# Convolution sums and gates of the odd layer kept in SBUF instead of DRAM, and the order of two key buffers swapped

## The chip, the cores and the metric

The kernel runs on one core of one Trainium2 chip. The metric is the device time of one execution in microseconds (us), the median of several runs. The profile beside it is of one execution of its own. Its engines are PE (TensorE, matmul), DVE (VectorE), ACT (ScalarE), POOL (GpSimd) and SP (SyncE, which here issues most DMA transfers, in the order of its own queue). Every engine runs its instructions in the order in which the program has them for that engine.

## What is computed

The reference is a backbone of two layers over 1024 latent tokens and 256 context tokens of width 1024. Layer 0 is attention. Layer 1, which the change touches, has two parallel branches: a convolution module and a neighbourhood attention. Cut to the convolution branch:

```
cv, cgl, cg, dq, dk, dv, dg = split_cols(h_lat @ w_in, ODD_WIDTHS)     # 7 x 512 columns
u = val * sigmoid(glu_gate)                                            # cv, cgl
u = conv(u, dw_w, 31 taps, depthwise, padding 15) + dw_b
u = silu(layer_norm(u, ln_g, ln_b))                                    # over the 512 channels
oc = u * silu(silu_gate)                                               # cg
...
od = neighbourhood attention of dq, dk, dv over a 16 x 64 grid, 8 heads, with context keys
y_lat = concatenate([oc, od * silu(dg)]) @ w_out
```

The result is x + gate * y_lat, normalised once more.

## The kernel before

Matrix products in 32-bit precision are made of three passes each: every operand is split into a high part (a cast on ACT) and a low part (a subtraction on POOL or DVE), and `mm3` (L327 to L329) multiplies high by high, low by high and high by low. A weight block is loaded raw by SP (L346, `wr`), cast on ACT (`wh`, L307) and split on POOL (`wl`, L310). Two raw slots serve a block of four pieces, so that pieces three and four can be loaded only when POOL has split pieces one and two.

Channels lie on the 128 partitions, tokens along the free axis. The 512 channels of the convolution are four tiles i = 0 to 3; the latent tokens are two chunks of 512.

Layer 1 runs in these stages.

- **Convolution stage** (pool `cv`). For each i, `conv_proj` multiplies for value, GLU gate and SiLU gate of both chunks. The gated value goes to `U` (1024 tokens and 15 zeros on each side); the SiLU gate goes through `silu2` (Tanh on ACT, one product on DVE) into `sgc`, and from there to the DRAM tensor `Gc` (L1050). `conv_steps` runs beside the matmuls (`pump`): 23 taps as multiply-adds on DVE in PSUM (`cps`), 8 taps on ACT and POOL (`cacc2`, `ptmp`), then a sum into `cacc`, the bias on ACT (L1073) and a store to the DRAM tensor `Uc` (L1074). After the four `conv_proj` comes `d_proj(0)`, the queries, keys, values and gate of the first two attention heads, whose results are stored to DRAM (`QD`, `KD`, `VD`, `GD`).
- **Normalisation stage** (pool `ln`). `ln_steps` normalises one chunk of 512 tokens over the 512 channels: it loads `uc` (4 tiles, 1 MB) from `Uc` (L1081), adds the four tiles on POOL (L1084 to L1086), gets the mean by a matmul with a constant (`mu`, L1091), subtracts it (L1095), squares and adds, gets the reciprocal root by two small groups of matmuls (`trs` and `bc`, L254 and L264), scales, applies SiLU (L1110 to L1114), loads the gate `gc` from `Gc` (L1109), multiplies (L1115) and stores to the DRAM tensor `Oc` (L1116). It runs beside the matmuls of `d_proj(1)`.
- **Attention stage** (pools `d0` and `d1`), woven with `d_proj(2)`, `d_proj(3)` and the output projection. `k_tiles` makes two pairs of key buffers: `KA`, loaded by DMA from `KD` (L384, L385), and `KB`, of which POOL sets four rows to 1.0 (L379) and ACT fills 64 rows by a copy out of `KA` (L390). Scores are a product with `KA` (L491) and one with `KB` (L495).

**What sets the order.** The program text gives each instruction a priority, by its place; the order on each engine is then made when the program is built, by a model of the time at which each instruction is ready. An instruction that is ready may go ahead of one with a higher priority that isn't. On the chip the order is fixed.

**Places in SBUF.** Pools are laid out as a stack, and inside a pool the tiles lie in the order of their first use. `cv` and `ln` begin at the same place, one after the other, and `d0` and `d1` follow at the same place again. A tile that takes the place of older ones waits for the last use of each of these. Bytes of one partition: `cv` 44,032 (taps 512, four U of 4,224, od_cs weights 14,336, cacc2, ptmp and cacc 4,096 each); `ln` with two uc of 8,192 and two gc of 2,048 within it; `d0` 34,880; each `KA` and `KB` 6,144. In layer 0 that part of the memory holds, among others, the residual stream `x1` of the output projection, in three chunks.

Of the kernel before, what the change touches and what calls it, by code (L numbers as in the profile page):

```python
# [10 lines left out]
F32 = mybir.dt.float32  # L11
F32R = mybir.dt.float32r
ALU = mybir.AluOpType
# [5 lines left out]
P = 128  # L19
DK = 8  # L20
NCTX = 256
NLAT = 1024
# [65 lines left out]
def tile_kernel(ctx: ExitStack, tc: tile.TileContext, a, out):  # L88
# [22 lines left out]
    def nm(s):  # L111
        uid[0] += 1
        return f"{s}_{uid[0]}"

    def dram(name, shape, dt=F32):
        return dp.tile(shape, dt, tag=name, name=name)
# [245 lines left out]
    def silu2(psrc, dst):  # L362

        SC.activation(dst, psrc, AF.Tanh, scale=0.5)
        VE.scalar_tensor_tensor(dst, dst, 1.0, psrc, op0=ALU.add, op1=ALU.mult)
# [8 lines left out]
            GP.memset(V[:, :, 128:192].bitcast(F32), 1.0)  # L374

    def k_tiles(pool, n, bufs=1):
        KA = pool.tile([P, n * P], F32R, tag="KA", name=nm("KAt"), bufs=bufs)
        KB = pool.tile([P, n * P], F32R, tag="KB", name=nm("KBt"), bufs=bufs)
        GP.memset(KB[64:68, :].bitcast(F32), 1.0)  # L379
        Ks.append((KA, KB))  # L380

# [608 lines left out]
    lng = const("lng", [P, 4])  # L990
    lnb = const("lnb", [P, 4])
    fg = const("fg", [P, DK])
    Gc = dram("Gc", [P, 4, NLAT])
    Oc = dram("Oc", [P, 4, NLAT])
    Uc = dram("Uc", [P, 4, NLAT])
    QD = [dram(f"QD{i}", [P, 2, 2, 512]) for i in range(4)]
    KD = [dram(f"KD{i}", [P, 2, 12 * P]) for i in range(4)]
    VD = [dram(f"VD{i}", [P, 12, 2, P]) for i in range(4)]
# [2 lines left out]
    with ExitStack() as l1x:  # L1001
# [11 lines left out]
        def half(name, tag="half"):  # L1013
            return lp.tile([P, 512], F32, tag=tag, name=nm(name), bufs=HALF[tag])
# [20 lines left out]
        def conv_proj(vp, i, U):  # L1035
            GP.memset(U[:, 0:15], 0.0)
            GP.memset(U[:, NLAT + 15 : NLAT + 30], 0.0)
            w = [load_w(wp, a["od_cv"], i, 256, WB), load_w(vp, a["od_cs"], i, 128, CWB // 2)]
            for c in (1, 2):
                t0, n = CHUNKS[c]  # L1040
                o = t0 - 256
                pv_ = yield from proj1(*w[0], 0, c)
                pg = yield from proj1(*w[0], 1, c)
                th = half("thc")
                SC.activation(th, pg, AF.Tanh, scale=0.5)
                VE.scalar_tensor_tensor(U[:, 15 + o : 15 + o + n], th, 1.0, pv_, op0=ALU.add, op1=ALU.mult)
                sg = half("sgc", "hf")
                pp = yield from proj1(*w[1], 0, c)
                silu2(pp, sg)
                SY.dma_start(Gc[:, i, o : o + n], sg)  # L1050

        def conv_steps(vp, i, U):
            ps2 = [bank("st", nm("cps")) for _ in range(2)]
            acc2 = vp.tile([P, NLAT], F32, tag="cacc2", name=nm("cacc2"), bufs=1)
            for k in range(31):
                u, w = U[:, k : k + NLAT], taps[:, i, k : k + 1]
                if k % 4 == 3:
                    t = acc2 if k == 3 else vp.tile([P, NLAT], F32, tag="ptmp", name=nm("ptmp"), bufs=1)
                    SC.activation(t, u, AF.Identity, scale=w)
                    if k > 3:  # L1060
                        GP.tensor_tensor(acc2, acc2, t, op=ALU.add)
                    continue
                for c, pc in enumerate(ps2):
                    uc = u[:, c * 512 : (c + 1) * 512]
                    if k == 0:
                        VE.tensor_scalar(pc, uc, w, None, op0=ALU.mult)
                    else:
                        VE.scalar_tensor_tensor(pc, uc, w, pc, op0=ALU.mult, op1=ALU.add)  # L1068
                yield
            acc = vp.tile([P, NLAT], F32, tag="cacc", name=nm("cacc"), bufs=1)  # L1070
            for c, pc in enumerate(ps2):
                VE.tensor_tensor(acc[:, c * 512 : (c + 1) * 512], pc, acc2[:, c * 512 : (c + 1) * 512], op=ALU.add)
            SC.activation(acc, acc, AF.Identity, bias=dwb[:, i : i + 1], scale=0.5)  # L1073
            SY.dma_start(Uc[:, i, :], acc)  # L1074
            yield

        def ln_steps(vp, c):

            cs = slice(c * 512, (c + 1) * 512)
            uc = vp.tile([P, 4, 512], F32, tag="uc", name=nm("uc"), bufs=2)  # L1080
            SY.dma_start(uc, Uc[:, :, cs])  # L1081
            s1 = vp.tile([P, 512], F32, tag="s1", name=nm("s1"), bufs=2)
            s2 = vp.tile([P, 512], F32, tag="s2", name=nm("s2"), bufs=1)
            GP.tensor_tensor(s1, uc[:, 0], uc[:, 1], op=ALU.add)  # L1084
            GP.tensor_tensor(s2, uc[:, 2], uc[:, 3], op=ALU.add)
            GP.tensor_tensor(s1, s1, s2, op=ALU.add)  # L1086
            yield
            for _ in range(2):
                yield
            mu = bank("st", nm("mu"))  # L1090
            PE.matmul(mu, ones5, s1, start=True, stop=True)  # L1091
            SC.copy(s2, mu)
            yield
            for i in range(4):
                VE.tensor_tensor(uc[:, i], uc[:, i], s2, op=ALU.subtract)  # L1095
                if i == 0:
                    SC.activation(s1, uc[:, i], AF.Square)
                else:
                    sq = vp.tile([P, 512], F32, tag="sql", name=nm("sql"), bufs=2)
                    SC.activation(sq, uc[:, i], AF.Square)  # L1100
                    VE.tensor_tensor(s1, s1, sq, op=ALU.add)
                yield
            yield
            bc = yield from rstd_steps(vp, [s1], 512, "st", 2.0)
            SC.copy(s2, bc)
            yield
            for i in range(4):
                gc = vp.tile([P, 512], F32, tag="gc", name=nm("gc"), bufs=2)
                SY.dma_start(gc, Gc[:, i, cs])  # L1109
                VE.scalar_tensor_tensor(uc[:, i], uc[:, i], lng[:, i : i + 1], s2, op0=ALU.mult, op1=ALU.mult)  # L1110
                th = vp.tile([P, 512], F32, tag="sql", name=nm("thl"), bufs=2)
                SC.activation(th, uc[:, i], AF.Tanh, scale=0.5, bias=lnbh[:, i : i + 1])
                VE.tensor_scalar(uc[:, i], uc[:, i], lnb[:, i : i + 1], None, op0=ALU.add)
                VE.scalar_tensor_tensor(uc[:, i], th, 1.0, uc[:, i], op0=ALU.add, op1=ALU.mult)  # L1114
                VE.scalar_tensor_tensor(uc[:, i], uc[:, i], 0.25, gc, op0=ALU.mult, op1=ALU.mult)  # L1115
                SY.dma_start(Oc[:, i, cs], uc[:, i])  # L1116
                yield

        def d_proj(i):
# [33 lines left out]
            for c in VORD:  # L1153
# [20 lines left out]
                for k0 in range(0, len(blocks), 4):  # L1174
# [11 lines left out]
                    while k < len(bl):  # L1186
# [3 lines left out]
                        SY.dma_start(VD[i][:, bl[k][0] : bl[k][0] + e - k], sv[:, k:e].bitcast(F32))  # L1190
                        k = e

        with tc.tile_pool(name="cv", bufs=1, reuse_waits="tile") as vp:
            stg[0] = vp
            taps = const("taps", [P, 4, 31], SY, vp)
# [17 lines left out]
        with tc.tile_pool(name="ln", bufs=1, reuse_waits="tile") as vp:  # L1213
# [12 lines left out]
            for _ in bg:  # L1226
                pass

        dlow = l1x.enter_context(tc.tile_pool(name="d0", bufs=1, reuse_waits="tile"))
        yo = dlow.tile([P, 3, 2, 512], F32, tag="yo", name="yo")  # L1230
        dpool = l1x.enter_context(tc.tile_pool(name="d1", bufs=1, reuse_waits="tile"))
# [362 lines left out]
```

## Time and profile before

| | |
|---|---|
| median of 3 runs | 1579.01 us (1578.08 to 1581.34) |
| the profiled execution | 1581.59 us |
| its span, first to last instruction | 1579.8 us |
| mean granted TensorE clock | 0.962 |
| DMA traffic | 208.23 MB, 132 GB/s on average |
| convolution stage | about 973 to 1137 us |
| normalisation stage | about 1137 to 1226 us |

The profile's page gives each engine's busy time; views of the trace group instructions by line, tile or stretch of time. In a waits view a line reads "engine, what it ran, <- what it waited for: us in total, times, longest". A granted clock of 1.00 is TensorE's full speed. A timeline's line is: start, us, engine, line, operation, what it writes and reads, count, and in brackets the idle time before it with what ended it. Names lose their digits there: the trace calls the tiles `s1` and `s2` both `s`, `p1` is `p`, `cacc2` is `cacc`.

### The profile page before, as it was taken

Reading aid. Unit: us, or ns where it says so; the run is one execution under the profiler, and the core shown is the slowest. Engines: PE = TensorE matmul, PEld = TensorE weight load, DVE = VectorE, ACT = ScalarE, POOL = GpSimd, SP = SyncE. Lnnn points to the kernel's source line nnn. Section 1 sums busy time; section 2 is a strip of 40 time slices with the busy share of each in tenths; the row PEclk is TensorE's granted clock in tenths of the full one; section 3 lists DMA queues with packets and bytes.
Section 4 is the critical chain, followed back from the end, with each engine's and each line's share of the span. In section 5 each row is a group of like instructions: output and inputs, shape, how many; then the busy total and the mean of one; then the engine's idle time right before and its main releaser. Section 6 shows DMA issues by size and latency. Waiting matters only on the chain.

```text
span 1579.8 us, 21684 instructions
## 1 busy us (share of the span) xinstructions
PE 1469.3 (93%) x7084; PEld 1172.7 (74%) x7084; DVE 1086.9 (69%) x2279; ACT 748.8 (47%) x1418; POOL 794.1 (50%) x637
## 2 busy tenths in 40 slices
PE   6899999998998999999999879999989999989995
PEld 2785987886886767876766657888877878768874
DVE  2833576588589865566677856999738466787866
ACT  3722333443435555447556654433334355554563
POOL 3531352553445666557556754664532244364665
PEclk8899999998999999999999989999999999979997
DMA  9473324422312253222112022222595577967632
GB/s 367 151 238 127 114 84 153 137 76 90 110 44 82 87 195 129 64 57 62 41 30 88 7 66 77 86 68 72 175 271 194 186 215 218 284 191 231 187 110 107
DMA packets 158105, 208.23 MB, mean 132 GB/s; under 512 B 15068, under 2 KB 96168, under 8 KB 157992
## 3 DMA queue, kind: packets, MB, share of 16 engines
q1 hardware_dynamic: 151328, 195.27, 39.1%
q10 hardware_dynamic: 6664, 11.57, 2.2%
q8 instruction: 56, 0.92, 0.3%
q14 instruction: 57, 0.47, 0.1%
HBM read 152.27 MB, written 53.22 MB: 130 GB/s over the span
## 4 chain that ended last, share of the span: by engine, by line
PE 73%; DVE 15%; DMA 6%; ACT 2%; issue 2%; POOL 1%; SPq 0%; ACTq 0%; DVEq 0%; POOLq 0%
PE p L327 6%; PE p L328 6%; PE p L329 6%; PE ov L447 4%; PE ov L449 4%; PE po L327 4%; PE po L329 4%; PE po L328 4%; PE ov L448 4%; PE st L491 4%; PE st L495 4%; PE pq L327 3%; PE pq L328 3%; PE pq L329 3%; PE pg L329 2%
## 5 line engine op out<-in xcount | busy, mean ns | idle before, releaser
L310 POOL TENSOR_TENSOR pl<-pf,ph 128x512 fp32r<-128x512 f32 (+4 forms) x321 | 392.9, 1235 | 362.8 <-ACT ph L307 280.0
L503 ACT ACTIVATE pf<-st 128x512 f32<-128x512 f32 x284 | 166.0, 596 | 213.7 <-PE st L495 159.2
L310 POOL TENSOR_TENSOR wl<-wr,wh 128x512 fp32r<-128x512 f32 (+2 forms) x131 | 168.7, 1300 | 187.8 <-ACT wh L307 145.9
L307 ACT CAST ph<-pf 128x512 fp32r<-128x512 f32 (+4 forms) x364 | 210.0, 588 | 19.6 <-PE ov L448 9.5
L327 PE MATMUL p<-hh,wh 128*128 128x512 f32 x448 | 180.0, 402 | 11.7 <-ACT wh L307 6.2
L328 PE MATMUL p<-hl,wh 128*128 128x512 f32 x448 | 179.6, 402 | 1.2 <-POOL hl L310 1.2
L329 PE MATMUL p<-hh,wl 128*128 128x512 f32 x448 | 176.3, 399 | 0.0
L491 PE MATMUL st<-QH,KAt 128*128 128x512 f32 (+4 forms) x364 | 142.5, 392 | 7.6 <-DVE pf L500 4.7
L447 PE MATMUL ov<-ph,Vt 128*128 128x512 f32 (+4 forms) x364 | 141.9, 390 | 5.5 <-DVE y L652 3.4
L449 PE MATMUL ov<-pl,Vt 128*128 128x512 f32 (+4 forms) x364 | 142.5, 391 | 4.5 <-POOL pl L310 3.5
L448 PE MATMUL ov<-ph,Vt 128*64 128x512 f32 (+4 forms) x364 | 139.9, 384 | 0.0
L495 PE MATMUL st<-QL,KBt 68*128 68x512 f32 (+4 forms) x364 | 135.8, 386 | 0.0
L307 ACT CAST wh<-wr 128x512 fp32r<-128x512 f32 (+2 forms) x134 | 80.8, 612 | 98.4 <-PE p L328 21.2
L1068 DVE SCALAR_TENSOR_TENSOR cps<-U,taps,cps 128x512 f32<-128x512 f32 x184 | 126.3, 749 | 0.9
L327 PEld LDWEIGHTS p<-hh,wh 128*128 128x128 f32 x448 | 85.4, 191 | 33.0 <-ACT wh L307 7.1
L615 DVE TENSOR_REDUCE mp<-mx 128x1 f32<-128x512 f32 x128 | 85.7, 682 | 25.7 <-PE mx L614 25.2
L328 PEld LDWEIGHTS p<-hl,wh 128*128 128x128 f32 x448 | 85.5, 191 | 21.7 <-POOL hl L310 2.2
L329 PEld LDWEIGHTS p<-hh,wl 128*128 128x128 f32 x448 | 85.3, 190 | 20.6 <-issue 0.5
L449 PEld LDWEIGHTS ov<-pl,Vt 128*128 128x128 f32 x364 | 70.5, 194 | 28.9 <-POOL pl L310 9.9
L327 PE MATMUL pq<-wh,hh 128*128 128x384 f32 x256 | 88.5, 346 | 2.8 <-ACT hh L307 2.8
L491 PEld LDWEIGHTS st<-QH,KAt 128*128 128x128 f32 x364 | 70.0, 192 | 26.3 <-ACT pf L503 6.9
L329 PE MATMUL pq<-wh,hl 128*128 128x384 f32 x256 | 87.4, 341 | 0.0
(277 smaller groups left out, 3482.6 us busy)
## 6 DMA issues: line engine op xcount, KB each, us to landing
mw<-in_mod_w_dram SPq DMA_DIRECT2D x16, 1024.0 KB, 5.7
Q<-qs SPq DMA_DIRECT2D x40, 256.0 KB, 2.1
QH<-Q SPq DMA_DIRECT2D x80, 128.0 KB, 2.7
mw<-in_mod_w_dram SPq DMA_DIRECT2D x16, 512.0 KB, 6.5
wr<-in_od_d_dram SPq DMA_DIRECT2D x32, 256.0 KB, 2.9
wr<-in_ev_qkv_dram SPq DMA_DIRECT2D x16, 384.0 KB, 5.1
KAt<-KD SPq DMA_DIRECT2D x16, 384.0 KB, 5.8
wr<-in_od_wo_dram SPq DMA_DIRECT2D x22, 256.0 KB, 3.3
```

Source lines behind the costliest of these rows:

```text
L307: acts.append(SC.copy(hi, src))
L310: (GP if leng == "g" else VE).tensor_tensor(lo, src, hi.bitcast(F32), op=ALU.subtract)
L327: PE.matmul(o, lh, rh, start=first, stop=False)
L328: PE.matmul(o, lh, rl, start=False, stop=False)
L329: PE.matmul(o, ll, rh, start=False, stop=last)
L447: PE.matmul(o, V[:, 64:192], ph[:, :n], start=(t == 0), stop=False)
L448: PE.matmul(g.ov[0:64, q0 : q0 + n], V[:, 0:64], ph[:, :n], start=False, stop=False)
L449: PE.matmul(o, V[:, 64:192], pl[:, :n], start=False, stop=(last and g.sink is None))
L491: sts.append(PE.matmul(st[:, :n], KA[:, cs], g.QH[:, q0 : q0 + n], start=True, stop=False))
L495: PE.matmul(st[:, :n], KB[0:68, cs], g.QL[0:68, q0 : q0 + n], start=False, stop=True)
L503: acts.append(SC.activation(pf[:, :n], st[:, :n], AF.Exp, scale=1.0 if g.bias else SCALE))
L1068: VE.scalar_tensor_tensor(pc, uc, w, pc, op0=ALU.mult, op1=ALU.add)
```

## The change

The DRAM tensors `Gc` and `Uc` are removed. A new pool `cu`, opened ahead of `cv` and closed after `ln`, holds two tiles of 16,384 bytes a partition: `ucs`, the convolution sums, and `gcs`, the gates. `silu2` writes into `gcs`; L1073's activation writes into `ucs`; `ln_steps` works on `ucs` in place and reads the gate in `gcs`. `k_tiles` takes `KB` before `KA`.

```diff
     def k_tiles(pool, n, bufs=1):
+        KB = pool.tile([P, n * P], F32R, tag="KB", name=nm("KBt"), bufs=bufs)
         KA = pool.tile([P, n * P], F32R, tag="KA", name=nm("KAt"), bufs=bufs)
-        KB = pool.tile([P, n * P], F32R, tag="KB", name=nm("KBt"), bufs=bufs)
         GP.memset(KB[64:68, :].bitcast(F32), 1.0)
...
-    Gc = dram("Gc", [P, 4, NLAT])
     Oc = dram("Oc", [P, 4, NLAT])
-    Uc = dram("Uc", [P, 4, NLAT])
...
-                sg = half("sgc", "hf")
                 pp = yield from proj1(*w[1], 0, c)
-                silu2(pp, sg)
-                SY.dma_start(Gc[:, i, o : o + n], sg)
+                silu2(pp, gcs[:, i, o : o + n])
...
-            SC.activation(acc, acc, AF.Identity, bias=dwb[:, i : i + 1], scale=0.5)
-            SY.dma_start(Uc[:, i, :], acc)
+            SC.activation(ucs[:, i, :], acc, AF.Identity, bias=dwb[:, i : i + 1], scale=0.5)
...
-            uc = vp.tile([P, 4, 512], F32, tag="uc", name=nm("uc"), bufs=2)
-            SY.dma_start(uc, Uc[:, :, cs])
+            uc = ucs[:, :, cs]
...
-                gc = vp.tile([P, 512], F32, tag="gc", name=nm("gc"), bufs=2)
-                SY.dma_start(gc, Gc[:, i, cs])
...
-                VE.scalar_tensor_tensor(uc[:, i], uc[:, i], 0.25, gc, op0=ALU.mult, op1=ALU.mult)
+                VE.scalar_tensor_tensor(uc[:, i], uc[:, i], 0.25, gcs[:, i, cs], op0=ALU.mult, op1=ALU.mult)
...
+        cux = ExitStack()
+        cup = cux.enter_context(tc.tile_pool(name="cu", bufs=1, reuse_waits="tile"))
+        ucs = cup.tile([P, 4, NLAT], F32, tag="ucs", name="uc")
+        gcs = cup.tile([P, 4, NLAT], F32, tag="gcs", name="gc")
         with tc.tile_pool(name="cv", bufs=1, reuse_waits="tile") as vp:
...
             for _ in bg:
                 pass
 
+        cux.close()
         dlow = l1x.enter_context(tc.tile_pool(name="d0", bufs=1, reuse_waits="tile"))
```

## The prediction

> **What bounds the kernel now.** The page first: the engine totals, then the chain that ended last.
>
> ```profile
> PE 1469.3 (93%) x7084; PEld 1172.7 (74%) x7084; DVE 1086.9 (69%) x2279; ACT 748.8 (47%) x1418; POOL 794.1 (50%) x637
> ...
> PE 73%; DVE 15%; DMA 6%; ACT 2%; issue 2%; POOL 1%; SPq 0%; ACTq 0%; DVEq 0%; POOLq 0%
> ```
>
> PE is busy nearly everywhere, so an edit pays only where PE stops, or where it runs at a low clock. The windows view over the stages that the edit touches shows where that is (columns: stretch, length, busy time and count for PE, PEld, DVE, ACT, POOL, granted clock, DMA share, GB/s).
>
> ```profile
> 1080.00:1100.00 20.00, 20.00 (x87) 16.02 (x86) 18.66 (x30) 7.58 (x11) 7.48 (x5) 1.00 0.24 73
> ...
> 1155.50:1161.00 5.50, 1.05 (x4) 0.21 (x2) 0.00 (x0) 0.69 (x2) 1.26 (x1) 0.86 1.01 290
> 1161.00:1166.50 5.50, 5.50 (x13) 4.31 (x14) 4.88 (x5) 3.03 (x6) 2.97 (x2) 0.52 1.04 229
> 1221.00:1224.30 3.30, 0.74 (x5) 0.35 (x3) 2.48 (x6) 0.60 (x1) 0.00 (x0) 1.00 0.86 271
> 1224.30:1227.60 3.30, 3.30 (x8) 2.62 (x9) 2.17 (x7) 0.00 (x0) 0.00 (x0) 0.50 0.99 324
> ```
>
> In the convolution stage (one window of several alike) PE is full at clock 1.00: nothing that the edit takes off ACT, DVE, SP or the DMA engines there can show. In the normalisation stage there are two holes. Hole A: PE stops in 1155.5 to 1161.0 and then runs 5.50 us at clock 0.52. Hole B: it stops in 1221.0 to 1224.3 and then runs 3.30 us at 0.50. The waits view, PE alone, 1130 to 1250, names what ended them:
>
> ```profile
> PE p L327 <- ACT wh L307: 4.5, 1, 4.5
> PE p L327 <- DVE spq L1128: 2.6, 1, 2.6
> PE bc L264 <- DVE nr L244: 0.7, 1, 0.7
> ```
>
> A is worth 4.5 + 5.50 x (1 - 0.52) = 7.1 us, B 2.6 + 3.30 x (1 - 0.50) = 4.2 us. The chain of waits through A, in order of time (start, us, what):
>
> ```profile
> 1137.32 3.16 DMA Uc<-cacc
> 1140.49 5.81 DMA uc<-Uc
> 1146.37 1.29 POOL s L1084
> ...
> 1148.68 11.55 DMA wr<-in_od_d_dram
> 1160.31 0.63 ACT wh L307
> ```
>
> PE starves for the second half of a weight block of d_proj(1). Its raw load was issued at 1148.68 and took 11.55 us to land. Everything ahead of it in this list is the round trip that the change removes. Two things made the load late, in the timeline of SP's queue (start, us from first to last, line, what):
>
> ```profile
> 1140.49 0.58 SPq L1081 DMA_DIRECT2D uc<-Uc  x1
> 1141.12 1.08 SPq L1109 DMA_DIRECT2D gc<-Gc  x2
> ...
> 1143.20 1.67 SPq L1190 DMA_DIRECT2D VD<-spv  x3
> 1144.92 0.61 SPq L1081 DMA_DIRECT2D uc<-Uc  x1
> 1146.32 0.50 SPq L384 DMA_DIRECT2D KAt<-KD  x1
> ...
> 1148.68 0.34 SPq L346 DMA_DIRECT2D wr<-in_od_d_dram  x1
> ```
>
> SP issues in order: the weight load stands behind two uc loads and two gc loads. And these put 2 x 1024 KB and 2 x 256 KB into DMA engines that are full, as the DMA view of 1130 to 1250 has them (count, KB each, median us to landing):
>
> ```profile
> uc<-Uc SPq DMA_DIRECT2D x2, 1024.0 KB, 8.8
> gc<-Gc SPq DMA_DIRECT2D x8, 256.0 KB, 3.9
> ...
> KAt<-KD SPq DMA_DIRECT2D x4, 384.0 KB, 10.2
> ```
>
> **Part 1, Uc and Gc are gone.** 4 Uc stores, 8 Gc stores, 2 uc loads and 8 gc loads, 22 transfers and 2 MB of each kind, leave SP's queue. Those of the convolution stage cost nothing today and give nothing, by the full window above. Arithmetic does not change: L1073 writes another place (4 on ACT), silu2's two writes go to gcs, L1115 reads gcs.
>
> In the normalisation stage the first sum on POOL (L1084) no longer waits for 3.16 + 5.81 us of DRAM traffic. It can start when the last L1073 ends (first row, the tile view of cacc: duration and first and last start), at about 1136.7, and POOL was idle then (second row, its timeline):
>
> ```profile
> L1073 ACT ACTIVATE cacc<-cacc,dwb x4: 1140/1148/1172, 1018.3 to 1135.5; 128x1024 f32<-128x1024 f32 x4
> 1142.41 2.55 POOL L310 TENSOR_TENSOR wl<-wr,wh 128x512 fp32r<-128x512 f32 x2 [11.87 <-PE p L328]
> ```
>
> Its three additions (1.29 each, 3.9 us) end at about 1140.6, ahead of these two splits. The raw slots of the weight block are freed by the splits, the first at 1143.7. In SP's queue the load then stands behind GD, VD and KAt alone: without the uc and gc issues, (0.58 + 1.08 + 0.61) us of issuing, it goes out at about 1146 or before. Ahead of it in the DMA engines remain GD (128x512 words, 256 KB), VD (six blocks of 128 KB) and two KAt (384 KB each), 1.8 MB. At the 290 GB/s of the window above that is 6.3 us, so it lands at about 1152, and cast (0.62) and split (1.3) are done by 1154. PE ran out at about 1156.5 (1.05 us of work in the window from 1155.5). So I take A as gone, with 2.5 us in hand: **7.1 us**, bounds 2 (a stop of 2.6 stays, with its slow stretch) and 7.1.
>
> A rule of the Trainium skill bears on how much of A comes back if a part of the stop stays: "TensorE: Matmul & The Clock Gate", Part 1, has the clock fall only after an idle window of about 3.4 us. By it a stop cut to 2.6 us would cost 2.6 and no slow stretch, and A's lower bound would be 4.5 instead of 2. The trace disagrees: hole B is a stop of 2.56 us, and the clock behind it was 0.50. I count with the trace.
>
> **Hole B** is DVE's tail of the second normalisation chunk. The timeline of DVE, and from the tile view of gc what DVE lost to these loads in all:
>
> ```profile
> 1221.31 0.69 DVE L1114 SCALAR_TENSOR_TENSOR uc<-thl,uc 128x512 f32<-128x512 f32 x1
> 1222.78 0.69 DVE L1115 SCALAR_TENSOR_TENSOR uc<-uc,gc 128x512 f32<-128x512 f32 x1 [0.78 <-DMA gc<-Gc]
> 1223.39 0.75 DVE L1128 SCALAR_TENSOR_TENSOR spq<-p,spq 128x256 fp32r<-128x256 f32 x2
> ...
>   DMA gc<-Gc: 3.2, 3
> ```
>
> PE waits for the bank that spq frees; spq stands behind L1115, which waited 0.78 us for a gc load. That wait goes. But this tail hangs on the second chunk's statistics, whose matmuls sit behind d_proj(1)'s own on PE. When A goes, d_proj(1) and the tail move forward together, and B mostly keeps its place between them. It gains the 0.78, and whatever the first chunk's DVE work (whose own gc waits also go, 3.2 us in three waits in all) no longer pushes into the second. It could also lose: if the program's order puts all of L1115 ahead of spq, one more of them (0.69 each) stands before it. Bounds: -1.5 (two more L1115) and +4.2 (B gone). I take **+1.5**, the gc wait and 0.7 of the 1.65 of slow stretch, nearer to B's staying than to either end.
>
> **Part 2, the places move.** cu takes 2 x 16,384 bytes of each partition where cv stood, so cv and ln lie 32,768 bytes higher. By the tile sizes, U 1 to 3 and the raw tiles of od_cs now lie on the third chunk's x1 of layer 0, which is in use until its last normalisation step. Before, two od_cs loads went out early (timeline of SP, then of POOL, then the chain of waits, where PE's run in the second conv chunk starts):
>
> ```profile
> 950.86 0.93 SPq L346 DMA_DIRECT2D wr<-in_od_cs_dram  x2
> ...
> 973.01 1.52 POOL L310 TENSOR_TENSOR wl<-wr,wh 128x256 fp32r<-128x256 f32 x2
> 977.24 3.95 POOL L310 TENSOR_TENSOR wl<-wr,wh 128x512 fp32r<-128x512 f32 x4 [2.71 <-ACT wh L307]
> ...
> 968.46 0.79 PE p L328
> ```
>
> Now they go out at about 973.5, and two more behind their splits at about 977. With an estimated 2.5 us to land (the smaller loads before them), half a split for the cast and 0.76 for the split, the gate weights are complete at about 981, some 2 us later than now. PE has 48 matmuls for the second conv chunk from 968.5 on, at 20.00/87 = 0.23 us each and the first of them at the slow 5.50/13 = 0.42: enough until about 981. Bounds 0 and -3; I take **-0.7**, nearer to the covered end. The queue behind these loads on SP, the next od_cv block, is not needed before that.
>
> **Part 3, key buffers.** d0 is 34,880 bytes (yo, ph, pl, pf, r1, r8, rb), so the d1 pool starts 2,112 bytes above cu's end, in ln's place; ln is 11,104 bytes. KB, taken first now with 2 x 6,144 bytes, covers the rest of it; KA lies clear of ln, so its loads (from 1146.32) wait for cv alone as before. What is new: the memsets of KB must wait for the last reads of s1, s2 and the sql tiles, where they ran far ahead, and ACT's copy into KB waits as well. The timelines of POOL and ACT, and the tile view of KBt, show what stands around them:
>
> ```profile
> 1126.90 2.69 POOL L379 MEMSET KBt<- 4x1536 f32 x2
> ...
> 1206.31 2.53 POOL L310 TENSOR_TENSOR wl<-wr,wh 128x512 fp32r<-128x512 f32 x2
> ...
> 1213.07 1.46 POOL L310 TENSOR_TENSOR wl<-wr,wh 128x512 fp32r<-128x512 f32 x1 [0.24 <-ACT wh L307]
> 1239.17 2.54 POOL L310 TENSOR_TENSOR wl<-wr,wh 128x512 fp32r<-128x512 f32 x2 [24.63 <-DMA bm<-in_d_bm_dram]
> ...
> 1212.85 1.48 ACT L390 CAST KBt<-KAt 64x1536 fp32r<-64x1536 f32 x1
> ...
> L495 PE MATMUL st<-QL,KBt x7: 276/325/401, 1242.9 to 1257.0; 68*128 68x512 f32 x3, 68*128 68x256 f32 x1, 68*128 68x352 f32 x1, 68*128 68x320 f32 x1
> ```
>
> What needs KB is the first L495 matmul, at 1242.9, and POOL is idle before 1239.17: put there, the memsets (2.69) and the copy (1.48) cost **0**. If that cover fails, see the slower rival. The attention's pf, ph and pl lay on uc and gc before and lie on ucs and gcs now: no new wait of size.
>
> **Sum.** 7.1 + 1.5 - 0.7 + 0 = 7.9 us. The profiled execution took 1581.59 (span 1579.8), 0.2% over the median of 1579.01, so on its own time the sum gives 1573.7, and against the median, unscaled, 1579.0 - 7.9 = **1571.1 us**. Later stages are full or wait for things the edit does not touch; a reordering there I bound at 2 us either way.
>
> **Rivals.**
> - *The weight load is hidden no better.* The program's order may put the attention's first loads (bm, bs, KAt) ahead of it, now that they are ready sooner, and the DMA engines stay full. For it: their share is 1.01 in hole A, and bm, bs and KAt already mix with it. Against it: 2.5 MB of uc and gc that filled them are gone. It leaves a stop of 2.6 or more: gain 2 + 1.5 - 0.7, or less; 1576 to 1580.
> - *Slower: KB's memsets hold POOL.* One place: POOL's queue at about 1206. If the memsets stand ahead of the four splits at 1206.31 to 1213.07, POOL stops until ln's last read of the sql tiles, L1114 at 1221.3 to 1222.0, and PE, which uses these splits within a few us, stops for about 12 us, with 2.6 of slow clock behind it. Net 7.9 - 14.6: 1586. It decides as soon as one memset stands before the second pair of splits (a stop near 8 then, about even). Against it: the order is made with the normalisation's readiness in view, and 24.6 us of idle POOL follow.
> - *Both holes close:* 7.1 + 4.2 + 0.7, less 0 to 0.7: 1567 to 1568.
>
> **Chances.** Forecast (A closes, B about as now; 1569 to 1574) 0.50; both close 0.18; load no better hidden 0.19; slower rival or another disturbance of the order of that size 0.13. About 3.2 us (0.2%) is what a measurement can tell from no change. Of the third case three quarters lie within it and the rest is faster; the last case is slower but for 0.01. That gives faster 0.73, same 0.15, slower 0.12. The range leaves out the slower rival's upper part and a little below: 1565.0 to 1580.5.
>
> **What would show it.** Right: no stop of PE between 1145 and 1165 and clock 1.00 there; wr of d_proj(1) landing within 7 us; L1084 on POOL near 1137; a PE hole of 1 to 3 us still at the end of the normalisation; KB's memsets after the last L310 split of that stage. Wrong: POOL stopped before those splits with a memset next; PE waiting for od_cs weights near 975 to 985; a stop of PE for wh that outlives uc and gc.

## The result, and the profile after

The changed kernel takes 1572.93 us (median of 8 runs, 1571.23 to 1577.62) against 1579.26 us for the kernel before on the same chip: a ratio of 0.9962, 95% interval [0.9951, 0.9974]. Run again on another chip it took 1572.99 against 1580.32, 0.9945 [0.9929, 0.996]. The forecast was 1571.1, most likely between 1569 and 1574. The time came out there, but the outer range put on record, 1565.0 to 1580.5, holds the kernel before's 1579.26 as well, so the time alone confirms little. Some of the steps behind it were wrong, and they are what the experiments are about.

The profiled execution of the changed kernel is the slowest of its 8 runs (1577.62, span 1575.8). It was already 2.7 us late at 918 us, in layer 0, which the change leaves alone. So times of the two traces are not compared directly below: the n-th matmul of one trace is set against the n-th of the other, and only what a stage adds to that difference counts.

Line numbers behind L1000 have moved by 3 to 8: L1069 is the bias on ACT (before: L1073), L1107 the product with the gate (L1115), L1120 `spq` (L1128), L1182 the VD store (L1190); L1141 is the KD store, L1256, L1266 and L1279 load bm, bs and V. The experiments' traces count their own lines, a few more or less; the tiles' names tell which is which.

The page of the changed kernel, totals and chain, shows hardly anything:

```profile
PE 1470.2 (93%) x7084; PEld 1173.2 (74%) x7084; DVE 1082.4 (69%) x2279; ACT 749.9 (48%) x1418; POOL 794.3 (50%) x637
...
PE 74%; DVE 15%; DMA 5%; ACT 2%; issue 2%; POOL 1%; SPq 0%; ACTq 0%; DVEq 0%; POOLq 0%
```

Its windows (stretch, length, busy time and count of PE, PEld, DVE, ACT and POOL, granted clock, DMA share, GB/s) show the place:

```profile
1080.00:1100.00 20.00, 20.00 (x87) 16.10 (x87) 19.01 (x30) 6.01 (x9) 9.93 (x6) 1.00 0.19 54
1145.00:1157.00 12.00, 12.00 (x61) 9.64 (x60) 6.65 (x10) 5.65 (x11) 5.12 (x4) 1.00 0.69 209
1157.00:1165.00 8.00, 8.00 (x36) 6.46 (x35) 1.51 (x4) 1.50 (x3) 0.00 (x0) 1.00 0.48 164
1214.90:1216.90 2.00, 0.26 (x2) 0.07 (x1) 2.00 (x5) 0.60 (x1) 2.00 (x2) 1.00 1.04 255
1216.90:1220.00 3.10, 3.10 (x14) 2.50 (x15) 0.47 (x2) 1.47 (x1) 1.07 (x3) 1.00 0.88 254
1235.00:1237.40 2.40, 0.50 (x3) 0.09 (x1) 0.42 (x1) 0.37 (x1) 0.00 (x0) 1.00 1.06 389
1237.40:1242.00 4.60, 4.60 (x15) 3.44 (x16) 0.89 (x4) 0.82 (x2) 1.28 (x1) 0.63 0.66 225
```

Hole A is gone: PE is full from 1145 to 1165 at clock 1.00. Hole B is a stop of 1.7 us near 1215 without a slow stretch. And there is a new one, called hole C below: PE stops near 1235 and then runs 4.60 us at clock 0.63. The waits view, PE alone, 1130 to 1250, names both:

```profile
PE p L327 <- DVE spk L310: 1.9, 1, 1.9
PE p L327 <- DVE spq L1120: 1.7, 1, 1.7
```

SP's timeline of the changed kernel shows what went as forecast, and what did not:

```profile
1145.44 1.81 SPq L1182 DMA_DIRECT2D VD<-spv  x3
1147.34 0.41 SPq L346 DMA_DIRECT2D wr<-in_od_d_dram  x1
...
1213.69 0.49 SPq L384 DMA_DIRECT2D KAt<-KD  x1
...
1218.20 1.98 SPq L1256 DMA_DIRECT2D bm<-in_d_bm_dram  x2
```

The weight load goes out with no KAt load ahead of it, and lands 4.4 us later (11.55 before). The first KAt load, which stood at 1146.32 before, goes out at 1213.69, and bm, bs and V follow it. The chain of waits into hole C (start, us, what) starts there:

```profile
1223.10 5.84 DMA KAt<-KD
...
1229.01 7.27 DMA KD<-spk
...
1236.43 0.38 ACT spk L307
...
1236.84 0.44 DVE spk L310
...
1237.32 0.50 PE p L327
```

The keys of d_proj(2) are split into `spk`, whose slot is free when the store of the last keys to KD has landed. That store took 7.27 us between the attention's loads; ACT's cast, DVE's split and PE waited for it in turn.

### The profile page after: what moved, and what is told of

Same layout as the page of the kernel before. It is cut to its first block, busy times and chain, and to the rows that moved or that the text cites. A ratio compares the mean times of both kernels' runs of the same rounds, so it can differ in the third digit from the quotient of the medians.

```text
span 1575.8 us, 21631 instructions
## 1 busy us (share of the span) xinstructions
PE 1470.2 (93%) x7084; PEld 1173.2 (74%) x7084; DVE 1082.4 (69%) x2279; ACT 749.9 (48%) x1418; POOL 794.3 (50%) x637
## 4 chain that ended last, share of the span: by engine, by line
PE 74%; DVE 15%; DMA 5%; ACT 2%; issue 2%; POOL 1%; SPq 0%; ACTq 0%; DVEq 0%; POOLq 0%
PE p L327 6%; PE p L329 6%; PE p L328 6%; PE ov L447 4%; PE ov L449 4%; PE ov L448 4%; PE po L327 4%; PE po L328 4%; PE po L329 4%; PE st L491 4%; PE st L495 3%; PE pq L327 3%; PE pq L329 3%; PE pq L328 3%; PE pg L329 2%; PE pm L179 2%
## 5 line engine op out<-in xcount | busy, mean ns | idle before, releaser
L447 PEld LDWEIGHTS ov<-ph,Vt 128*128 128x128 f32 x364 | 71.4, 196 | 25.5 <-ACT ph L307 4.5
```

Source lines behind the costliest of these rows:

```text
L447: PE.matmul(o, V[:, 64:192], ph[:, :n], start=(t == 0), stop=False)
```

## The experiments

The table sets every kernel's trace against that of the kernel before, by the number of the matmul: what the difference grew by in each stage, in us, less is faster. Matmul 4300 is at 953 us of the kernel before, 4400 at 979, 5100 at 1139, 5400 at 1206, 5600 at 1250, 6400 at 1422; the last is 7083. Medians are against the kernel before's of the same chip.

| kernel | front, 4300-4400 | A, 5100-5400 | B and C, 5400-5600 | attention, 5600-6400 | rest | median, ratio [interval] |
|---|---|---|---|---|---|---|
| changed kernel | +1.3 | -7.5 | +0.8 | +0.4 | -0.4 | 1572.93, 0.9962 [0.9951, 0.9974] |
| e11, the same again | +1.2 | -7.5 | +0.6 | +0.9 | -0.2 | 1572.99, 0.9945 [0.9929, 0.996] |
| e1, KA first | +1.3 | -7.5 | +1.5 | -0.2 | +1.1 | 1575.4, 0.9974 [0.9963, 0.9985] |
| e2, V in the lower pool | +1.2 | -6.7 | -2.3 | +0.3 | -0.9 | 1570.85, 0.994 [0.9926, 0.9953] |
| e12, e2 again | +1.3 | -7.1 | -2.3 | +1.0 | -1.0 | 1571.72, 0.9941 [0.9928, 0.9953] |
| e3, sums only | -0.2 | -3.8 | -1.0 | +6.2 | 0.0 | 1577.94, 0.9987 [0.9978, 0.9995] |
| e4, gates only | -0.1 | -7.2 | +3.5 | -1.6 | +7.2 | 1581.83, 1.0011 [1.0002, 1.002] |
| e5, 2 MB of traffic added | +1.2 | -7.6 | +0.1 | -2.1 | 0.0 | 1572.36, 0.9954 [0.9939, 0.9969] |
| e6, e2 and the traffic | +1.2 | +0.8 | -4.9 | +2.8 | +0.8 | 1579.52, 1.0 [0.9988, 1.0013] |
| e7, e2, attention's loads late | +1.1 | -7.6 | +1.1 | +1.2 | +0.6 | 1577.45, 0.9978 [0.9965, 0.999] |
| e8, e2 and a pad | 0.0 | -7.0 | -2.3 | +2.4 | -0.9 | 1572.21, 0.9949 [0.9935, 0.9963] |
| e9, before, attention's loads late | -0.1 | -4.1 | +2.2 | +3.6 | +0.5 | 1580.17, 1.0001 [0.999, 1.0013] |
| e10, e2, pad, loads near 1155 | -0.2 | -7.6 | -5.0 | +0.3 | +1.9 | 1569.05, 0.9925 [0.991, 0.994] |

The two pairs of repeats (changed kernel and e11, e2 and e12) show how far these columns can be read: they agree within 0.7 us. Behind matmul 5100 the order of the matmuls differs from kernel to kernel. Counted with the median time of each shape, all kernels have done the same work by matmul 5400 (within 0.1 us), but by 5600 the changed kernel, e11, e1, e4 and e5 have done 0.5 us more than the kernel before: by so much their column for B and C reads too high, and the one for the attention too low.

### The order of KA and KB (e1)

```diff
     def k_tiles(pool, n, bufs=1):
-        KB = pool.tile(...)
         KA = pool.tile(...)
+        KB = pool.tile(...)
```

> The changed kernel with KA taken before KB again, so that KA and not KB lies in the normalisation's place. Theory (the attention's first loads go out late in the changed kernel because the whole d1 pool, whichever buffer is first, is laid out behind the normalisation's place in the built order): KA's first load again near 1214, PE's stop near 1235 stays at about 2 us with a slow stretch, time within 2 us of the changed kernel, 1571 to 1575. Rival (which of the two buffers lies there matters, since a DMA load with a real wait on the normalisation replaces a memset with one): KA's load some us later, the stop grows, 1576 to 1580.

With KA first again, hole A closes just as well (-7.5), and the first KAt load is as late as in the changed kernel (SP's timeline of e1):

```profile
1211.92 0.49 SPq L384 DMA_DIRECT2D KAt<-KD  x1
```

So the swap does not bring the loads forward or back. The first buffers of `d1` lie in the place of `ln` in either order, and the loads of all that are allocated behind them go out late. That the one is the reason of the other is inferred, here and below: it fits the kernels that leave the loads to the build (early before the change and in e2 and e3, where nothing of `d1` lies on the normalisation; late in e1, e4 and e5, where its first buffer does), but no trace shows the build making that choice. The median of e1 lies 0.4 above the range expected. KB first is about 2 us better in the median, a difference that the intervals do not quite separate.

### The attention's loads clear of the normalisation (e2, repeated as e12)

```diff
-        v_tiles(dpool, 7, 2)
+        v_tiles(dlow, 7, 2)
```

The V buffers move into `d0`, so that `d1` starts past the end of `ln`.

> The changed kernel with the two value buffers (10,752 bytes) taken from the pool d0 instead of d1: d1 then begins past the normalisation's place, KA and KB are both clear of it. Theory (the stop of PE near 1235 with its slow stretch, 3.7 us in all, comes from KA, bm, bs and V all being loaded between 1213 and 1233): KA, bm and bs go out near 1140, the stop near 1235 is gone, 1568 to 1571. Rival (the earlier stop near 1156 closed because these loads had left its stretch, not because of uc): some 2.5 MB of KA, bm and bs stand ahead of the weight load again and 2 to 7 us of that stop come back, 1571 to 1577.

The loads are early again, ahead of the weight load (SP's timeline of e2):

```profile
1138.14 0.49 SPq L384 DMA_DIRECT2D KAt<-KD  x1
...
1149.24 0.33 SPq L346 DMA_DIRECT2D wr<-in_od_d_dram  x1
```

The waits view of PE, 1130 to 1250, has no wait for `spk` left: hole C is closed, and B and C together are 2.5 to 2.7 us better than in the changed kernel, the 0.5 us of work taken off. In its place 0.6 us of hole A is back (0.3 in e12):

```profile
PE p L327 <- DVE spq L1120: 1.5, 1, 1.5
PE bc L264 <- DVE nr L244: 1.1, 1, 1.1
PE p L327 <- ACT wh L307: 0.6, 1, 0.6
```

Side by side on one chip, the repeats stand at 1571.72 (e12) and 1572.99 (e11):

> The version with V in the lower pool (e2) again, on the chip of the changed kernel's repeat. If the early loads of the attention are worth what hole C cost less the rest of hole A, it is 1 to 3 us below the changed kernel, 1569 to 1572; if hole C is not the kernel's, the two are within 1 us.

> The changed kernel again, beside the next one on one chip. Its profiled execution lay 4.7 above its median, 2.65 of it in layer 0. If hole C (stop of 1.9 near 1235, 3.7 lost) belongs to the kernel, it is there again within 1 us, and the time is 1572 to 1575; if it was that execution's, it is gone and the end stands 6 to 9 us ahead of the kernel before, from the same point in layer 0.

Hole C is the kernel's, not that one execution's: PE waits 1.8 us for `spk` in e11 too, and the stage columns repeat. The gain of e2 over the changed kernel is 1.3 us in the medians on one chip (e12 against e11) and 2.1 across two chips, with overlapping intervals.

### Half of the change each (e3, e4)

e3 keeps the sums in SBUF and sends the gates through DRAM; e4 does it the other way round. Each undoes its half of the diff:

```diff
 # e3
-                silu2(pp, gcs[:, i, o : o + n])
+                sg = half("sgc", "hf")
+                silu2(pp, sg)
+                SY.dma_start(Gc[:, i, o : o + n], sg)
...
+                SY.dma_start(gc, Gc[:, i, cs])
 # e4
-            SC.activation(ucs[:, i, :], acc, AF.Identity, bias=dwb[:, i : i + 1], scale=0.5)
+            SC.activation(acc, acc, AF.Identity, bias=dwb[:, i : i + 1], scale=0.5)
+            SY.dma_start(Uc[:, i, :], acc)
...
+            SY.dma_start(uc, Uc[:, :, cs])
```

> Only the sums stay in SBUF; the gates go through DRAM as before (8 stores, 8 loads). The normalisation's pool then ends below the first key buffer. Theory (the round trip of uc is what opened the stop near 1156; gates cost only the 0.8 us wait of DVE at its end): no stop near 1156, loads of the attention early, no stop near 1235, 1569 to 1573. Rival (traffic of any kind ahead of the weight load opens the stop): KA, bm, bs and two gc loads, some 3 MB, stand ahead of it, a stop of 2 to 5 us near 1156 with its slow stretch, 1573 to 1579.

> Only the gates stay in SBUF; the sums go through DRAM as before (4 stores, 2 loads of 1 MB). Theory (the round trip of uc is the cause of the stop near 1156): the weight load goes out behind both uc loads again and the stop stays at 2 to 5 us, and the attention's loads are late as in the changed kernel: 1576 to 1581. Rival (traffic of the attention's loads was the larger part): these have left the stretch, 2 MB of uc alone land in time, no stop near 1156, 1571 to 1575.

Neither half is worth the change, and e4's median lies above both ranges. e4 is the one to look at: the round trip of the sums is back, and hole A is closed all the same. SP's timeline of e4:

```profile
1140.98 1.25 SPq L1078 DMA_DIRECT2D uc<-Uc  x2
...
1144.91 0.94 SPq L346 DMA_DIRECT2D wr<-in_od_d_dram  x2
```

The weight load takes 10.1 us to land, nearly as long as before. But it is issued at 1144.91 instead of 1148.68, since no KAt load stands ahead of it (these are late in e4 as well, near 1218) and no gate load either. So the round trip of the sums does not open hole A by itself. What e4 lost lies elsewhere: +3.5 at the end of the normalisation, and 7.2 behind matmul 6400, where PE waits 5.2 us at 1549 for ACT's cast of the attention's result (0.3 in the kernel before). This was not followed further.

In e3 the attention's loads are early again (the first KAt load at 1133.44), and two gate loads stand ahead of them. PE stops 1.2 us for `wh` and runs slow behind it, so of hole A only 3.8 is gained. Then e3 loses 6.2 in the attention stage, though PE's idle time there is only 0.8 us longer in all. The windows of that stage, the kernel before's and then e3's, show what it was:

```profile
1250.19:1421.88 171.69, 159.81 (x802) 130.38 (x800) 117.01 (x276) 93.26 (x184) 77.44 (x71) 0.95 0.76 224
1240.52:1418.39 177.87, 165.22 (x802) 133.41 (x800) 119.26 (x280) 92.83 (x184) 76.43 (x70) 0.92 0.74 216
```

The granted clock falls from 0.95 to 0.92. By the clock's records PE ran at 0.50 for 27.3 us of this stage instead of 17.1, and half of these 10.2 us, 5.1, is most of the 6.2.

### Traffic without a wait (e5, e6)

```diff
             uc = ucs[:, :, cs]
+            SY.dma_start(Oc[:, :, cs], ucs[:, :, 512:1024])
```

Two stores of 1 MB; in e5 on the changed kernel, in e6 on e2.

> The changed kernel, with two stores of 1 MB each (sums of the second half of the tokens, to the DRAM tensor Oc, where the true values overwrite them later) issued by SP at the two points where the kernel before had its uc loads. Nothing waits for them but the later Oc stores. The attention's first loads are still late, as in the changed kernel. Theory 1 (hole A needs two backlogs ahead of the weight load, the 2.5 MB of uc and gc and the attention's early 2.7 MB of KA, bm and bs): one of them alone does not open it; PE's stop near 1155 stays under 1 us, and the time is that of the changed kernel, 1571 to 1575. Theory 2 (the 2 MB of uc and gc traffic alone starve the weight load): the stop comes back with 3 to 4.5 us and a slow stretch, 1576 to 1580.

> The version with V in the lower pool (e2, attention's first loads early again), with the same two stores of 1 MB. Now both backlogs stand ahead of the weight load of d_proj(1), but no instruction waits for a round trip of the sums. Theory 1 (backlog in the DMA engines): hole A opens again, the weight load takes 9 us or more to land, PE stops 2.5 to 5 us near 1155 and runs at about half clock behind it; 1574 to 1578. Theory 3 (the wait of the first POOL sum for the round trip, by which the splits that free the raw slots come late): the first sum starts near 1137 here, the stop stays under 1.5 us, and the time is that of e2, 1570 to 1573.

e5: the traffic alone costs nothing, and the weight load lands in 4.6 us. Its two stores go out together at 1138.02, in the time of the kernel before some 3 us ahead of the first uc load there, so e4 is the stricter case of the two. The attention's loads are as late in e5 as in the changed kernel (the first KAt load at 1212.52), and yet hole C is not there: PE waits 2.5 us for `spq` and never for `spk`. So late loads need not open hole C. What holds is that B and C together do better with the loads early (e2, e12, e8) than late (the changed kernel, e11, e1, e5).

e6: with the traffic and the attention's early loads together, the gain at A is gone (+0.8 for -6.7 of e2), though no sum waits for a round trip. The windows of e6:

```profile
1150.00:1157.00 7.00, 7.00 (x36) 5.78 (x34) 4.48 (x7) 2.54 (x5) 0.00 (x0) 1.00 1.05 322
1157.00:1160.00 3.00, 0.85 (x5) 0.67 (x5) 0.49 (x2) 0.37 (x1) 0.53 (x1) 0.89 1.03 261
1160.00:1166.00 6.00, 5.70 (x24) 4.57 (x23) 0.86 (x4) 1.11 (x3) 1.30 (x2) 0.77 0.93 241
```

Its chain of waits:

```profile
1148.13 8.41 DMA GD<-sgd
...
1156.62 7.85 DMA wr<-in_od_d_dram
```

The DMA engines are full, a 256 KB store takes 8.41 us, by the chain the weight load goes out only when that has landed, and it takes 7.85. Expected were 9 us or more, and one stop of 2.5 to 5 for the weight. PE stopped 2.2 for `spv`, whose slot waits for a store, with a slow stretch behind it, and then only 0.3 for the weight; two more stops of 1.3, at 1179 and 1184, were not followed. Theory 3 is out: the first sum starts at 1139.95, which is 1136.8 in the time of the kernel before, and the time is not that of e2 (it is 1.5 above the range of theory 1). So the backlog is enough to undo the gain, but e6 does not show hole A itself again: its order of matmuls is another, and PE runs out of something else first. Hole B shrinks to a wait of 0.2 there (-4.9).

### The kernel before, with the attention's loads late (e9)

```diff
+                    if i == 1 and not qst:
+                        qst.append(st)            # the first QD store of d_proj(1)
...
-            load_k(hd, KD[i][ds, 0, :], KD[i][ds, 1, :])
+            with tc.issue_after(qst[0].ins):
+                load_k(hd, KD[i][ds, 0, :], KD[i][ds, 1, :])
```

and the same around the loads of bm and bs. Uc and Gc stay.

> The kernel before (sums and gates through DRAM, as it was), with nothing changed but the place of the attention's first loads in SP's queue: KA, bm and bs go out behind the first QD store of d_proj(1). Theory 1 (hole A is the weight load behind two backlogs in the DMA engines; taking either away closes it): PE's stop of 4.5 near 1156 falls under 1 us, the weight load lands in 7 us or less although the round trip of the sums is still ahead of it, and 5 to 7 us of the change's gain come without the change: 1572 to 1575. Theory 3 (the round trip of the sums delays the weight load by itself): the stop stays at 2.5 or more; 1576 to 1580.

Theory 1 is right about the stop, which falls to 0.4 us (matmuls 5100 to 5200 gain 6.5), though the load takes 9.6 us and not 7 or less; and it is wrong about the time: the median is that of the kernel before. DVE's timeline of e9 shows where a part of it went, 2.2 by the table:

```profile
1209.96 1.28 DVE L1114 SCALAR_TENSOR_TENSOR uc<-thl,uc 128x512 f32<-128x512 f32 x2
1215.83 1.34 DVE L1115 SCALAR_TENSOR_TENSOR uc<-uc,gc 128x512 f32<-128x512 f32 x2 [4.59 <-DMA gc<-Gc]
1217.08 0.75 DVE L1130 SCALAR_TENSOR_TENSOR spq<-p,spq 128x256 fp32r<-128x256 f32 x2
```

and SP's why:

```profile
1200.64 9.46 SPq L346 DMA_DIRECT2D wr<-in_od_d_dram  x4
1210.19 0.86 SPq L1116 DMA_DIRECT2D Oc<-uc  x2
1211.10 1.10 SPq L1109 DMA_DIRECT2D gc<-Gc  x2
```

The last two gate loads stand in SP's queue behind four weight loads and two stores, DVE waits 4.59 us for them where it waited 0.78 before, `spq` stands behind, and PE stops 4.3 us (2.6 before). Behind A, this kernel also gives 2.4 back between matmuls 5200 and 5400 (a weight load 8.9 us on its way between the moved loads) and 3.6 in the attention stage. There PE's idle time is that of the kernel before, but the clock is lower again (0.95 there), at 0.50 for 23.9 us instead of 17.1:

```profile
1245.04:1420.31 175.27, 163.42 (x801) 132.41 (x800) 121.72 (x283) 94.14 (x185) 77.62 (x70) 0.93 0.74 221
```

### Two further versions, and the front (e7, e8, e10)

e7 is e2 with the attention's loads put, by the same means as in e9, behind the first Oc store. e8 is e2 with a pad that moves the raw tiles of od_cs past the end of x1's third chunk:

```diff
             U = ...
+            if i == 0:
+                GP.memset(vp.tile([P, 512], F32, tag="pad", name="pad"), 0.0)
             w = [load_w(wp, a["od_cv"], i, 256, WB), load_w(vp, a["od_cs"], i, 128, CWB // 2)]
```

> The version with V in the lower pool (e2), with the attention's first loads (KA, bm, bs) put behind the first Oc store in SP's queue, near 1181, where the DMA share was between 0.3 and 0.5. Theory 1: with neither backlog ahead of the weight load, the stop of 0.64 near 1157 goes, the load lands in under 5 us, and hole C (stop near 1235 of the changed kernel) stays closed, since these loads are in before 1212; 1569 to 1571, 0.5 to 1.5 below e2. Rival: these loads meet the weight loads of 1184 to 1203, and what is gained at A is lost there, or the attention begins late; 1571 to 1574.

> The version with V in the lower pool (e2), with a pad of 2048 bytes a partition behind the first U, so that the raw tiles of od_cs lie clear of the third chunk of x1 (POOL sets the pad to 0.0, one instruction more). The order of SP's queue is that of e2. Theory (the place): the two od_cs loads go out near 950 again instead of 971, and PE's stop of 1.03 near 974 goes; about 1.0 to 1.3 below e2, 1569.5 to 1570. Rival (the stop comes from the order of the casts or splits at the stage's start, not from the place): the stop stays at 0.8 or more, 1570.5 to 1571.5.

e7 is the miss, above both ranges. Hole A closes to the last bit (-7.6), but its loads, out from 1182 to 1192, meet the stores and weights of d_proj(2). The windows of e7:

```profile
1180.00:1199.00 19.00, 19.00 (x102) 15.74 (x101) 12.35 (x22) 7.03 (x14) 1.93 (x2) 1.00 0.89 222
1199.00:1203.00 4.00, 0.56 (x6) 0.36 (x4) 0.57 (x3) 1.01 (x3) 0.04 (x1) 1.00 0.99 367
1203.00:1209.00 6.00, 6.00 (x23) 4.77 (x24) 3.18 (x4) 2.95 (x7) 3.76 (x3) 0.72 0.39 138
```

In e8 the two od_cs loads go out at 950 again, as before the change (SP's timeline of e8: four loads, of which the last waits until 975), and PE's waits from 966 to 985 have no line for `wh`, where the changed kernel has one of 1.2:

```profile
949.84 25.23 SPq L346 DMA_DIRECT2D wr<-in_od_cs_dram  x4
```

The front costs 1.1 to 1.3 us in each of the eight rows that have both tiles in `cu` and no pad, and nothing in the other five. The median of e8, above both ranges, does not show that 1.3: +2.4 in the attention stage stands against it, where PE ran 6.8 us more at clock 0.50 than in the kernel before.

e10 takes both, and puts the loads behind the first QD store of d_proj(1) instead, near 1155:

> The changed kernel with V in the lower pool, the pad of 2048 bytes ahead of the raw tiles of od_cs, and KA, bm and bs behind the first QD store of d_proj(1), near 1158: each of the three stops named so far (front 1.0, hole A's rest of 0.6, hole C) has its cause taken away, and the loads go out earlier than in e7, where their 1182 to 1192 met the weights of d_proj(2). Theory 1: no stop near 974, none in 1140 to 1190, no slow stretch before 1212; 1568.5 to 1571. Rival (these loads meet some other weight load, as in e7): a stop of 2 us or more between 1190 and 1240 grows; 1572 to 1577.

It is the fastest of all: 1569.05, 0.9925 [0.991, 0.994]. It makes three edits at once, and its interval overlaps that of e12 beside it. PE has no wait of the profile's list between 1130 and 1260. Its windows:

```profile
1145.00:1165.00 20.00, 20.00 (x101) 16.66 (x100) 7.37 (x15) 6.39 (x13) 4.21 (x4) 1.00 0.67 191
1200.00:1220.00 20.00, 19.93 (x90) 15.86 (x89) 12.88 (x28) 4.75 (x8) 5.17 (x4) 1.00 0.74 236
1220.00:1240.00 20.00, 20.00 (x110) 17.06 (x109) 8.93 (x23) 11.41 (x24) 9.96 (x9) 1.00 0.61 185
```

Hole B closes here too, worth 5.0 with the bc wait. Why e10 closes it and e2 does not was not separated: in e10 the first score matmul of the attention already stands at 1195.6, so PE has other work while DVE finishes the normalisation.

## Why the prediction held, and where it did not

**Hole A, 7.1 taken, 7.5 measured.** It closes in both traces of the changed kernel. The forecast said out at about 1146 or before, landing at about 1152; set to the time of the kernel before (by matmul 5100) it went out at 1144.4 and landed at 1148.8. The margin is wider than forecast for a reason that the forecast did not have: the two KAt loads that it left ahead of the weight had gone too.

**Its cause was put too narrowly.** The prediction says that everything ahead of the weight load in the chain is the round trip. The chain is true, and one of two sufficient remedies. What decides is when the load lands. Issue and landing, in time of the kernel before:

| kernel | ahead of the weight load | out | us to landing | landed | PE's stop |
|---|---|---|---|---|---|
| before | uc, gc, KA | 1148.7 | 11.6 | 1160.2 | 4.5 |
| e6 | 2 MB of stores, KA, bm, bs | 1153.5 | 7.8 | 1161.3 | 2.2 for `spv`, 0.3 for the weight |
| e2 | KA, bm, bs | 1148.4 | 7.6 | 1156.0 | 0.6 |
| e3 | KA, bm, bs, gc | 1150.5 | 6.7 | 1157.2 | 1.2 |
| e9 | uc, gc | 1146.5 | 9.6 | 1156.1 | 0.4 |
| e4 | uc | 1144.4 | 10.1 | 1154.5 | none |
| e5 | 2 MB of stores | 1145.4 | 4.6 | 1150.0 | none |
| changed | neither | 1144.4 | 4.4 | 1148.8 | none |

PE runs out of work near 1156 (in e6, with its other order of matmuls, of `spv` and not yet of the weight). With both lots of transfers ahead, the load lands at 1160 to 1161, 4 to 5 us later; with the attention's loads and only the gates (e3), 1 us later; with either lot alone it lands in time or misses by half a microsecond. The change takes one lot away by its main part and the other, unmeant, by the place of the tiles.

**The failed step: "KA lies clear of ln, so its loads (from 1146.32) wait for cv alone as before".** They went out at 1213.69. That KA's own place is clear of `ln` was not the point: KA is allocated behind KB, KB's place waits for the normalisation, and the loads of everything behind it (KA, bm, bs, V) stand late in SP's order. The order of the loads is seen; that the allocation makes it is the inference named under e1. The price fell on the term for B. Taken was **+1.5**, inside bounds of -1.5 and +4.2. B alone gained 2.8 (from -4.62 to -7.46 between matmuls 5400 and 5500), and hole C, which no part of the forecast had, took 3.7 back. Both together cost 0.6 to 0.8 by the table, and 0.1 to 0.3 with the 0.5 us of earlier work taken off. With the loads early, the same stage gains 2.3 (e2, e12), and 5.0 in e10.

**B and the gate loads.** The prediction let the gc wait of 0.78 go, and no more. e9 shows what they can cost: with A closed and the gates still in DRAM, DVE's wait for gc grows from 0.78 to 4.59 and PE's stop for `spq` from 2.6 to 4.3, and of the 6.5 us gained at A the tail takes 2.2 back. e3, with the gates in DRAM and A partly closed, does not repeat it: its longest wait for gc is 1.5, and its B and C gain 1.0. So the gates in SBUF can keep a part of A's gain; that the two halves of the change need each other is not shown. The losses of e3 (the clock) and e4 (behind matmul 6400) lie elsewhere.

**The front, -0.7 taken, -1.2 to -1.3 measured in the changed kernel.** The mechanism was right, by e8: it is the place of the od_cs tiles on x1. The first two loads went out where the forecast had them (973.3 and 973.7 in the time of the kernel before). But the work of PE did not cover them until 981: it stopped at 974.7 for the cast of the first weights, which the prediction had named as a sign of being wrong. The size was taken nearer to the covered end, and lay within the bounds.

**KB's memsets, 0, right.** They stand behind the last splits of the stage, in a stretch of POOL that was idle before and after (POOL's timeline of the changed kernel):

```profile
1207.44 2.72 POOL L310 TENSOR_TENSOR wl<-wr,wh 128x512 fp32r<-128x512 f32 x2 [3.53 <-ACT wh L307]
1214.39 2.69 POOL L379 MEMSET KBt<- 4x1536 f32 x2 [4.23 <-DVE uc L1106]
1217.14 0.90 POOL L374 MEMSET Vt<- 128x448 f32 x2
1230.86 2.55 POOL L310 TENSOR_TENSOR wl<-wr,wh 128x512 fp32r<-128x512 f32 x2 [12.83 <-PE p L329]
```

The slower rival had the right wait (for L1106, the last read of the `sql` tiles) and the wrong neighbour: no split stands behind it.

**Later stages, "a reordering there I bound at 2 us either way".** For the changed kernel the attention and the rest came to 0.0 and +0.7. As a bound it is too small: e3's attention stage lost 6.2, most of it by the clock, and e4's end 7.2, with edits of the same kind.

**The sum.** 7.5 - 0.7 (B and C) - 1.25 - 0.4 (the rest, mean of two) = about 5.2 by the traces, where the forecast had 7.9; the medians say 6.3 and 7.3. The term for B was 2.2 off, the front 0.55 and the later stages 0.4, less 0.4 more at A: these are the 2.7 us. So the near hit rests on A, and the other terms were small beside it rather than right. 1 to 2 us between traces and medians stay unexplained. Single executions differ by more than that: up to matmul 4300, which no edit here touches, the thirteen traces of the table lie between 5.0 us ahead of and 1.9 us behind the kernel before's.

## What to carry to other kernels

A late load has a queue ahead of it, and each part of that queue may be the one to remove: work out when the load lands without each of them, before one is called the cause. When buffers change places, follow not only the tile that overlaps but every tile allocated behind it, since their first loads may stand behind its wait. And where one hole is closed, look for the next load that the same tail waits for: in e9 the gate loads took back 2.2 of the 6.5 us that the first hole gave. Before a loss in a later stage is put down to an edit, look at the granted clock there.

## What the hardware showed unexpectedly

How long a stop lowers the clock was less plain than the prediction had it: the stop of 1.7 us near 1215 in the changed kernel left the clock at 1.00, the one of 1.9 us near 1235 did not. In each of the fourteen traces every change of the granted clock lies on a grid of 3.41 us, and the clock is 1.00 or 0.50 in each window of that grid; the 0.52, 0.63 and 0.72 above are means over stretches that take in both. What goes with a low clock is how little PE worked in the window before. The kernel before's hole B, then the changed kernel's holes B and C, cut along the grid:

```profile
1220.91:1224.32 3.41, 0.85 (x5) 0.44 (x3) 2.59 (x6) 0.60 (x1) 0.00 (x0) 1.00 0.85 268
1224.32:1227.73 3.41, 3.41 (x8) 2.72 (x9) 2.15 (x7) 0.00 (x0) 0.00 (x0) 0.50 1.01 324
1214.50:1217.91 3.41, 1.67 (x8) 1.08 (x7) 2.88 (x7) 0.91 (x2) 3.35 (x4) 1.00 1.00 275
1217.91:1221.32 3.41, 3.41 (x16) 2.76 (x15) 0.00 (x0) 1.47 (x1) 0.12 (x1) 1.00 0.94 294
1234.98:1238.39 3.41, 1.51 (x7) 0.90 (x7) 1.08 (x4) 0.37 (x1) 0.00 (x0) 1.00 0.98 362
1238.39:1241.80 3.41, 3.41 (x11) 2.43 (x9) 0.23 (x2) 0.62 (x2) 1.28 (x1) 0.50 0.66 216
```

A window with PE busy for 0.85 or 1.51 us is followed by one at 0.50, one with 1.67 is not. Over all fourteen traces, of the windows at full clock 159 of 162 with PE busy below 45% were followed by a low one, 78 of 364 between 45% and 80%, and 6 of 5426 above 80%. The Trainium skill, "TensorE: Matmul & The Clock Gate", Part 1, has the clock fall after an idle window of about 3.4 us. The length agrees with the 3.41 us here; that the window must be idle does not, since 1.51 us of work in it did not keep the clock up. So a stop of about 2 us may cost itself alone, or also half of a slow window, 1.7 us, by how it lies on the grid and how full the rest of its window is.
